# First attention's v and compressed rows at the right end, taken over by the first expert pair; five ring pairs in place of six

## The chip, the cores and the metric

The kernel runs on one core of a Trainium2 chip. Its engines work side by side: TensorE (PE) multiplies matrices, VectorE (DVE) and ScalarE (ACT) do elementwise work and read the matrix results out of PSUM, GpSimd (POOL) does small elementwise work, and SyncE (SP) issues nearly all transfers between HBM and the on-chip memory (SBUF), which 16 DMA engines carry out. The metric is the time of one execution in microseconds (us). Times of several runs are given as a median; a profiled execution has a time of its own.

## What is computed

One input of 256 tokens by 1024 features, float32, goes through two transformer blocks. The weights are read once from HBM. Cut to what matters here:

```python
# first block
h  = rms_norm(x);  z = h @ w_in                 # 1024 x 5664: c_q, c_kv, k_rope, dq, dk, dv, two gates
q  = rms_norm(c_q) @ w_uq;  k_nope, v = split(rms_norm(c_kv) @ w_ukv)
o_mla  = softmax(q k^T) v                        # 16 heads ("first attention")
o_diff = (softmax(q1 k1^T - bias) - lam * softmax(q2 k2^T - bias)) vd    # 8 heads ("second attention")
x  = x + (sigmoid(g_a) * o_mla + sigmoid(g_b) * o_diff) @ w_out
a  = softmax(rms_norm(x) @ router_w);  idx, gate = top_k(a^T, 32)        # 16 experts, 32 tokens each
x  = x + scatter(idx, gate * ((silu(xe @ w_gate) * (xe @ w_up)) @ w_down))   # w_*: 8.4 MB per expert each
# second block: projection, convolution, stick-breaking attention, gating unit, ffn of 4096, gated output
```

The experts' weights are 16 x 3 x 8.4 MB = 403 MB of the 490 MB that the kernel reads.

## The kernel before

The program is written with a framework that places tiles in SBUF, sets the waits and orders the instructions of each engine. In `build`, a block fixes the order on PE and POOL to the order of the text for the whole program; the others (DVE, ACT, SP) are ordered by the framework, by their place in the text and by when it expects them to be ready, except in marked blocks (`manual_schedule`). One of these covers the first projection in `mla` (DVE and ACT), one the last expert's down projection (SP too). Each engine then works through its instructions strictly in order; SP too, so an issue that waits holds up all that stand behind it.

SBUF is used from both ends: pools opened on the left stack up, pools with `side="right"` stack down from the other end, and a pool that is closed gives its place to the next one opened there; a tile placed on an old one waits until the old one's readers are done. The pools that matter, in the order in which they lie (KB per partition):

- left, for the whole program or long: `cp` (x and constants), `sm`, `fa` (32 KB: xh, xl, o_mla, o_diff), `qk` (24 KB: q and k of the first attention, then the gates `gT`, then weights);
- left, in the front only: `wsp` (three pairs of split weights of 1088 columns, 25.5 KB), `fs` (small statistics), `fd` (16 KB: d0 and d1, the second attention's q and k), `fv` (13 KB: pos_r, dist, lr, tab and the first attention's v of 8 KB), `a1` to `a3` (transposed heads, biases, logits, probabilities), `fe` (8 KB: first `ch`, the split and transposed compressed rows, later d2, the second attention's v), `a4`;
- right, in the front: `ring1`, four slots of 8 KB through which the front's weights pass;
- right, from the experts on: two slots of 16 KB where the four were, `pp` of 8 KB, and six slots `ring2` of 16 KB, which lie over the front's left pools.

The front (`front`, `mla`, `diff`) multiplies in three passes: each weight piece is split into a rounded part and the rest (`split`, `put`: one ACT cast, one DVE subtraction) and multiplied three times (`mm3`). `look` keeps `self.ahead` pieces split ahead. `tables` makes the position tables on POOL; `lam` makes the scalar lambda of the second attention from `lr`; `diff` ends with the gates, the merges, `w_out` and the router's logits; `route` picks the tokens.

In `experts` a weight pair is 2.1 MB (256 rows of w_gate or w_up, 512 rows of w_down): 12 pairs per expert, 192 in all, of which the last four are loaded as eight halves of 1.05 MB by `load`. `pload` takes the next place off the ring. If that is a pool, it goes back on the end of the ring, and the load waits for the matmuls that used the pair before; if it is a function, the place is used once, by one load of 2.1 MB or two of 1.05 MB, and does not come back:

```python
r = self.ring.pop(0)
if callable(r):
    hs = r()
else:
    self.ring.append(r)
    hs = [r.tile([128, 4096], F32, name="w", tag="w")]
```

`SLOTS` gives the first turn of the ring: a number is a slot of `ring2`, -1 one of the two wide slots, -2 the next place of `once`. The places of `once` are: xl with the upper part of `qk`; the lower 16 KB of `qk`; o_diff with o_mla. Before the change the first eleven pairs so take r2[3], once, r2[2], r2[1], once, r2[0], wide, wide, r2[4], r2[5], once, and the ring that remains has eight slots: r2[3], r2[2], r2[1], r2[0], wide, wide, r2[4], r2[5].

At the last expert (`e == 15`), after gate and up, three of the six slots are closed for the split weights of the second block; `load(0)` and `load(1)` load the two column halves of w_down, four quarters each, into the other three and into the first of them again. The two wide slots take the second block's first weights; a slot `ring3` is added after the experts and three more after the mixer.

## Time and profile before

| what | us |
|---|---|
| median of 3 runs | 1506.15 |
| lowest, highest of them | 1505.64, 1506.5 |
| the profiled execution | 1505.89 |
| its span, first to last instruction | 1504.2 |
| PE busy | 1138.1 |
| DVE busy | 475.5 |
| ACT busy | 354.8 |
| POOL busy | 133.0 |

The page cuts the span into 40 slices of 37.6 us and prints the busy share of each engine in tenths, the mean busy share of the 16 DMA engines, and the GB/s that they moved; below it follow the chain of work that ended last and the costliest groups of instructions. A row of the timeline is one instruction or a run of like ones on an engine: start, duration, engine, line of the program, what it writes and reads, how many, and in brackets how long the engine stood before and what ended that. "SPq" is SP's queue: its rows are the moments at which transfers are issued, not the transfers.

### The profile page before, as it was taken

The page shows a single profiled execution, that of the slowest core. Times are in us where ns is not written, and L with a number is a line of the kernel's source. Part 1 is how long each engine was busy: PE and PEld are TensorE (multiplying, and loading weights), DVE is VectorE, ACT ScalarE, POOL GpSimd, SP SyncE. Part 2 cuts the span into 40 slices and gives each one's busy share as a digit, 9 for nine tenths or more (in the row PEclk, how much of TensorE's full clock was granted, in tenths as well). Part 3 has the DMA queues.
Part 4 walks back from the last instruction along what each step waited for, and adds up shares of the span by engine and source line. Part 5 has one row for each costly group of instructions (what it writes and reads, how often), then busy time and mean ns, then how long its engine had stood idle before and what let it go on. Part 6 is the DMA issues. An engine that isn't in the chain of part 4 may idle for free.

```text
span 1504.2 us, 16611 instructions
## 1 busy us (share of the span) xinstructions
PE 1138.1 (76%) x6821; PEld 627.1 (42%) x6821; DVE 475.5 (32%) x969; ACT 354.8 (24%) x644; POOL 133.0 (9%) x181
## 2 busy tenths in 40 slices
PE   7999999885655566556565555656556899999998
PEld 6777897431111121111111111111111597889986
DVE  6987787410000000000000000000000477655456
ACT  5565655100000010000000000000000455554444
POOL 4613111000000000000000000000000134011010
PEclk9999999998688787887877888787877999999999
DMA  7533339999999999999999999999999972655520
GB/s 250 184 109 103 111 117 357 426 426 427 427 427 427 424 427 428 427 427 429 426 427 427 427 427 427 427 427 427 427 427 418 360 262 92 216 173 192 198 110 29
DMA packets 74842, 492.61 MB, mean 327 GB/s; under 512 B 5593, under 2 KB 10014, under 8 KB 50446
## 3 DMA queue, kind: packets, MB, share of 16 engines
q1 hardware_dynamic: 74366, 490.69, 80.7%
q8 instruction: 53, 0.87, 0.2%
q0 software_dynamic: 400, 0.86, 0.2%
q14 instruction: 23, 0.19, 0.0%
HBM read 490.48 MB, written 1.05 MB: 327 GB/s over the span
## 4 chain that ended last, share of the span: by engine, by line
DMA 50%; PE 37%; DVE 6%; issue 2%; ACT 1%; SPq 1%; POOL 1%; ACTq 0%; DVEq 0%
DMA w<-in_expert_w_down_dram 17%; DMA w<-in_expert_w_gate_dram 17%; DMA w<-in_expert_w_up_dram 15%; PE tr L1213 5%; PE mm L209 5%; PE mm L210 5%; PE mm L211 5%; PE acc L210 2%; PE acc L211 2%; PE acc L209 2%; DVE wl L121 2%; PE su L1261 2%; SPq L1280 1%; DMA w<-in_w_in_dram 1%; PE s L740 1%
## 5 line engine op out<-in xcount | busy, mean ns | idle before, releaser
L1213 PE MATMUL tr<-w,xe 128*32 128x512 f32 x2048 | 325.5, 768 | 207.3 <-DMA w<-in_expert_w_up_dram 121.6
L1213 PEld LDWEIGHTS tr<-w,xe 128*32 128x32 f32 x2048 | 64.7, 126 | 446.9 <-issue 162.6
L1261 PE MATMUL su<-w,hT 128*32 128x512 f32 x960 | 164.1, 821 | 92.3 <-DMA w<-in_expert_w_down_dram 84.4
L121 DVE TENSOR_TENSOR wl<-w,wh 128x1024 fp32r<-128x1024 f32 (+1 forms) x157 | 193.9, 1242 | 87.6 <-ACT wh L120 86.2
L120 ACT CAST wh<-w 128x1024 fp32r<-128x1024 f32 (+1 forms) x157 | 163.3, 1048 | 114.1 <-PE mm L211 44.9
L1239 DVE SCALAR_TENSOR_TENSOR hd<-tr,re,sg 128x512 f32<-128x512 f32 x16 | 12.0, 750 | 508.6 <-PE tr L1213 507.7
L1250 ACT ACTIVATE yh<-su,cols 128x512 fp32r<-128x512 f32 x17 | 11.7, 687 | 565.4 <-PE su L1261 528.8
L209 PE MATMUL mm<-xh,wh 128*128 128x256 f32 x448 | 128.7, 287 | 0.9 <-DVE x L1632 0.9
L210 PE MATMUL mm<-xh,wl 128*128 128x256 f32 x448 | 125.8, 281 | 0.0
L211 PE MATMUL mm<-xl,wh 128*128 128x256 f32 x448 | 125.8, 281 | 0.0
L1261 PEld LDWEIGHTS su<-w,hT 128*32 128x32 f32 x960 | 31.4, 132 | 209.4 <-DMA w<-in_expert_w_down_dram 134.3
L1251 DVE SCALAR_TENSOR_TENSOR yl<-su,cols,yh 128x512 fp32r<-128x512 f32 x17 | 12.8, 751 | 272.5 <-ACT yh L1250 272.5
L209 PEld LDWEIGHTS mm<-xh,wh 128*128 128x128 f32 x448 | 84.4, 188 | 4.0 <-issue 2.3
L210 PEld LDWEIGHTS mm<-xh,wl 128*128 128x128 f32 x448 | 84.5, 189 | 0.3
L211 PEld LDWEIGHTS mm<-xl,wh 128*128 128x128 f32 x448 | 84.4, 188 | 0.0
L1237 ACT ACTIVATE sg<-tr,re 128x512 f32<-128x512 f32 x16 | 11.0, 687 | 269.6 <-PE tr L1213 264.3
L209 PE MATMUL mm<-wh,xh 128*128 128x512 f32 (+1 forms) x140 | 57.7, 412 | 0.7 <-ACT wh L120 0.5
L1368 POOL TENSOR_SCALAR_AFFINE_SELECT m_gt<-ones 128x128 f32<-128x128 f32 x1 | 0.3, 287 | 647.6 <-DMA w<-in_expert_w_down_dram 647.6
L210 PE MATMUL mm<-wh,xl 128*128 128x512 f32 (+1 forms) x140 | 54.1, 386 | 0.0
L211 PE MATMUL mm<-wl,xh 128*128 128x512 f32 (+1 forms) x140 | 54.0, 385 | 0.0
L209 PE MATMUL acc<-wh,fhl 128*128 128x512 f32 x128 | 50.0, 391 | 0.0
L211 PE MATMUL acc<-wl,fhl 128*128 128x512 f32 x128 | 49.9, 390 | 0.0
(455 smaller groups left out, 1514.1 us busy)
## 6 DMA issues: line engine op xcount, KB each, us to landing
w<-in_expert_w_up_dram SPq DMA_DIRECT2D x64, 2048.0 KB
w<-in_expert_w_gate_dram SPq DMA_DIRECT2D x63, 2048.0 KB
w<-in_expert_w_down_dram SPq DMA_DIRECT2D x59, 2048.0 KB
w<-in_w_ff_dram SPq DMA_DIRECT2D x32, 1024.0 KB
w<-in_w_in_dram SPq DMA_DIRECT2D x29, 1024.0 KB
w<-in_expert_w_down_dram SPq DMA_DIRECT2D x10, 1024.0 KB
w<-in_w_out_dram SPq DMA_DIRECT2D x5, 1024.0 KB
w<-in_w_ple_gate_dram SPq DMA_DIRECT2D x4, 1024.0 KB
```

The lines of the kernel that those rows point to most:

```text
L120: self.nc.scalar.copy(h, src)
L121: (self.nc.gpsimd if pool else self.nc.vector).tensor_tensor(l, src, f(h), op=ALU.subtract)
L209: mm(out, ah, bh, start=start, stop=False, **kw)
L210: mm(out, al, bh, start=False, stop=False, **kw)
L211: mm(out, ah, bl, start=False, stop=stop, **kw)
L740: nc.tensor.matmul(S[:, t, :], qT[:, t * 128 : t * 128 + 128], kT, start=True, stop=True)
L1213: nc.tensor.matmul(ps[32 * j : 32 * j + 32, :], self.xe[k // 4][:, k % 4, 32 * e : 32 * e + 32], ws[k % 2][:, 0, 512 * j : 512 * j + 512], ...
L1239: nc.vector.scalar_tensor_tensor(hd, gu[1], re, sg, op0=ALU.mult, op1=ALU.mult)
L1250: nc.scalar.activation(yh, d, AF.Identity, scale=gate)
L1251: nc.vector.scalar_tensor_tensor(yl, d, gate, f(yh), op0=ALU.mult, op1=ALU.subtract)
L1261: nc.tensor.matmul(d[r : r + 32, :], hT[:, a, j, :], ws[a // 2][:, a % 2, 512 * b : 512 * b + 512], start=j == 0 and a < 2, stop=j == 3 an ...
L1280: nc.sync.dma_start(ws[j], A["expert_w_down"][0, 15, 512 * j : 512 * j + 512, 512 * b : 512 * b + 512].rearrange("(p a) n -> p a n", a=4))
```

## The change

Two pools `early` of 8 KB each are opened first on the right, and `pp` behind them, ahead of `ring1`. In the front, v lies in the first and `ch` in the second. When the experts' weights are loaded, the two are the first place of `once`: the first pair goes there in two halves of 1.05 MB. `ring2` has five slots; the first eleven pairs take early, once (xl with qk's part), r2[2], r2[1], once, r2[0], wide, wide, r2[3], r2[4], once, and the ring that remains has seven slots: r2[2], r2[1], r2[0], wide, wide, r2[3], r2[4]. At the last expert, r2[2] to r2[4] are closed and r2[0] and r2[1] stay. After the experts the two `early` pools join the ring of the second block in place of one `ring3`; after the mixer two `ring3` in place of three.

To make room, `lr` shares the place of pos_r, `lp` that of a transposed head, and the split buffers have 1024 columns, so that a weight tile of 544 columns is split row block by row block (eight pieces of 544 where there were four of 1088), with two pieces ahead in place of one.

```diff
--- before.py
+++ after.py
@@ -21,12 +21,12 @@
 PSUM = bass.MemoryType.PSUM
 
 
-R1, R2 = 4, 6
+R1, R2 = 4, 5
 
 LN_EXP = 6
 
-SLOTS = (3, -2, 2, 1, -2, 0, -1, -1, 4, 5, -2)
-WSPLIT = 1088
+SLOTS = (-2, -2, 2, 1, -2, 0, -1, -1, 3, 4, -2)
+WSPLIT = 1024
 AHEAD = 2
 T, D, NT = 256, 1024, 2
 EPS = 1e-6
@@ -310,6 +310,9 @@
         self.cms, self.wide = {}, set()
         self.cp = self.open("cp")
         self.sm = self.open("sm", 2)
+
+        self.early = [self.open("early", side="right") for _ in range(2)]
+        ppool = self.open("pp", side="right")
         r1 = self.ring = [self.open("ring1", side="right") for _ in range(R1)]
         r1 = list(r1)
         self.x = self.cp.tile([128, NT, D], F32, name="x")
@@ -325,7 +328,6 @@
             for r in reversed(r1):
                 self.close(r)
             r1 = [self.open("ring1", side="right") for _ in range(R1 // 2)]
-            ppool = self.open("pp", side="right")
             r2 = [self.open("ring2", side="right") for _ in range(R2)]
             self.wide = {id(r) for r in r1 + r2}
             once = self.once()
@@ -342,13 +344,13 @@
             ew = self.experts(rp, r2, ppool, late)
             if self.upto < 3:
                 return
-            self.ring.append(self.open("ring3", side="right"))
+            self.ring += self.early
             bm, self.ap = self.open("bm"), self.open("bq", 2)
             again = dict(ws="sg", wm="hd", ah="hT", u="yh", gl="yl", gv="sel")
             self.mix(Parts(bm, (ew, again)))
             self.close(self.ap)
             self.close(bm)
-            self.ring += [self.open("ring3", side="right") for _ in range(3)]
+            self.ring += [self.open("ring3", side="right") for _ in range(2)]
             self.ap = self.open("bf", 2)
             self.ps.turn("acc", "s", "s", "su", "o")
             self.ffn()
@@ -363,6 +365,7 @@
             both.append(tile(self.qp, "a", 4096))
             return [tile(self.fa, "xl"), tile(self.qp, "b")]
 
+        yield lambda: [tile(pool, "w") for pool in self.early]
         yield first
         yield lambda: both
         yield lambda: [tile(self.fa, "o_diff"), tile(self.fa, "o_mla")]
@@ -487,7 +490,7 @@
         wr = fp.tile([128, 2, 32], F32, name="wr")
         nc.sync.dma_start(wr[:, 0, :], A["mla_q_hnorm_w"][:, 64:].to_broadcast((128, 32)))
         nc.sync.dma_start(wr[:, 1, :], A["mla_k_hnorm_w"][:, 64:].to_broadcast((128, 32)))
-        self.lr = fp.tile([128, 4, 64], F32, name="lr")
+        self.lr = fp.tile([128, 4, 64], F32, name="lr", tag="pos_r")
         nc.sync.dma_start(self.lr, A["diff_lambda"].rearrange("o a b -> o (a b)").to_broadcast((128, 256)).rearrange(
             "p (a b) -> p a b", a=4))
 
@@ -518,7 +521,7 @@
                        allow_small_or_imprecise_dtypes=True)
         self.onr = cp.tile([16, 128], F32R, name="onr")
         nc.gpsimd.tensor_copy(self.onr, self.ones[:16, :])
-        lp = fp.tile([128, 2, 64], F32, name="lp")
+        lp = self.ap.tile([128, 2, 64], F32, name="lp", tag="qT", bufs=4)
         ls = fp.tile([128, 2], F32, name="ls")
         nc.vector.tensor_tensor(lp, lr[:, 0::2, :], lr[:, 1::2, :], op=ALU.mult)
         nc.vector.tensor_reduce(ls, lp, axis=AX.X, op=ALU.add)
@@ -573,8 +576,8 @@
         a1, a2, a3 = self.open("a1", 2), self.open("a2", 2), self.open("a3", 2)
         fe, a4 = self.open("fe"), self.open("a4", 2)
         same = lambda *tags: dict(zip(tags, tags))
-        self.fp = fb = Parts(fs, (fd, same("d0", "d1")), (fv, same("v", "dist", "tab", "pos_r", "lr")),
-                             (fe, same("d2")))
+        self.fp = fb = Parts(fs, (fd, same("d0", "d1")), (fv, same("dist", "tab", "pos_r")),
+                             (fe, same("d2")), (self.early[0], dict(v="w")), (self.early[1], dict(ch="w")))
         self.ap = Parts(a1, (a2, same("L")), (a3, same("P")), (a4, same("PT", "jj")))
         self.mla(fb)
         self.diff(fb)
@@ -601,7 +604,7 @@
             self.ahead = 0
             self.look()
             put(range(4, 8))
-            self.ahead = 1
+            self.ahead = 2
             ws = []
             tables = self.tables()
             for k in range(8):
@@ -621,7 +624,7 @@
                 pass
         self.ahead = AHEAD
         cn = fb.tile([128, NT, 512], F32, name="cn", tag="d1")
-        ch = fb.tile([128, 2, 4, T], F32R, name="ch", tag="d2")
+        ch = fb.tile([128, 2, 4, T], F32R, name="ch")
         h, l = ch[:, 0], ch[:, 1]
         self.transpose_split(cc, self.col["mla_q_norm_w"], h, l, range(4), ("tr", "o", "tr", "mm"))
         sc = self.sm.tile([128, 2, NT], F32, name="sc", tag="sc")
@@ -1223,7 +1226,7 @@
                 self.close(rp)
                 ew = self.open("ew")
             if e == 15:
-                for r in reversed(r2[3:]):
+                for r in reversed(r2[2:]):
                     self.close(r)
                     self.ring.remove(r)
                 self.wsp = self.open("wsp", 4)
@@ -1308,7 +1311,7 @@
             down(1, second, lambda j: self.fill(j % 2))
         self.fill(2)
         self.dump("x2", self.x)
-        for r in reversed(r2[:3]):
+        for r in reversed(r2[:2]):
             self.close(r)
         return ew
```

## Rows read from the trace of the kernel before

**Rows 1.** The page's slices: DMA engines busy in tenths, and GB/s.

```profile
DMA  7533339999999999999999999999999972655520
GB/s 250 184 109 103 111 117 357 426 426 427 427 427 427 424 427 428 427 427 429 426 427 427 427 427 427 427 427 427 427 427 418 360 262 92 216 173 192 198 110 29
```

**Rows 2.** The page's chain that ended last, shares of the span by engine.

```profile
DMA 50%; PE 37%; DVE 6%; issue 2%; ACT 1%; SPq 1%; POOL 1%; ACTq 0%; DVEq 0%
```

**Rows 3.** Windows: each engine's busy time, granted clock, DMA share, GB/s.

```profile
160.00:200.00 40.00, 38.94 (x320) 35.71 (x320) 32.70 (x94) 22.45 (x62) 5.97 (x4) 1.00 0.39 128
...
227.00:251.00 24.00, 24.00 (x115) 15.88 (x114) 19.19 (x43) 13.92 (x38) 5.96 (x8) 1.00 1.00 402
251.00:255.00 4.00, 3.95 (x15) 2.29 (x14) 2.34 (x6) 2.04 (x4) 0.00 (x0) 1.00 0.09 37
256.00:288.00 32.00, 27.83 (x162) 20.17 (x165) 16.09 (x55) 9.26 (x22) 0.00 (x0) 0.89 1.00 421
...
293.00:1163.00 870.00, 536.78 (x3182) 128.90 (x3174) 51.79 (x101) 28.01 (x41) 0.79 (x1) 0.80 1.01 427
```

**Rows 4.** SP's timeline, 0 to 300 us: start, duration, line, transfer, count.

```profile
48.30 0.50 SPq L334 DMA_DIRECT2D wpl<-in_w_ple_proj_dram  x1
54.47 133.35 SPq L104 DMA_DIRECT2D w<-in_w_in_dram  x16
227.02 0.35 SPq L294 DMA_DIRECT2D w<-in_expert_w_gate_dram  x1
...
254.38 0.33 SPq L299 DMA_DIRECT2D w<-in_expert_w_gate_dram  x1
282.62 0.33 SPq L294 DMA_DIRECT2D w<-in_expert_w_down_dram  x1
290.88 8.40 SPq L294 DMA_DIRECT2D w<-in_expert_w_gate_dram  x4
```

**Rows 5.** Waits of SP's queue, 195 to 300 us: total, times, longest.

```profile
SPq L299 <- DVE mhl L121: 17.3, 1, 17.3
```

**Rows 6.** PE's timeline at the first expert, 278 to 293 us.

```profile
279.43 1.06 PE L1213 MATMUL tr<-w,xe 128*32 128x512 f32 x8
...
289.75 1.07 PE L1213 MATMUL tr<-w,xe 128*32 128x512 f32 x8
```

**Rows 7.** Windows of 2 us after the pause, last column GB/s.

```profile
254.00:256.00 2.00, 2.00 (x8) 1.25 (x8) 1.48 (x3) 1.67 (x2) 0.00 (x0) 1.00 0.41 70
256.00:258.00 2.00, 2.00 (x9) 1.61 (x9) 2.00 (x3) 1.37 (x5) 0.00 (x0) 1.00 0.91 303
258.00:260.00 2.00, 2.00 (x14) 1.77 (x13) 0.39 (x2) 1.99 (x4) 0.00 (x0) 1.00 1.06 451
```

**Rows 8.** Chain that ended last, 505 to 560 us: start, us, what.

```profile
532.73 1.97 PE su L1261 x16
...
548.10 7.05 PE tr L1213 x64
```

**Rows 9.** Groups by line and form, 0 to 30 us: count, busy, mean ns.

```profile
L121 DVE TENSOR_TENSOR wl<-w,wh 128x1088 fp32r<-128x1088 f32 x4 | 5.1, 1290 | 3.0 <-ACT wh L120 3.0
```

**Rows 10.** POOL's timeline in the front, 22.9 to 25.5 us.

```profile
23.08 1.18 POOL L480 TENSOR_TENSOR di<-pos_r,pos_c 128x256 int32<-128x256 int32 x2
```

**Rows 11.** DVE's timeline in the front, 22.7 to 29 us.

```profile
25.04 0.16 DVE L528 SCALAR_TENSOR_TENSOR nlam<-ls 128x1 f32<-128x1 f32 x1 [2.22 <-ACT ls L525]
...
27.92 0.49 DVE L205 TENSOR_SCALAR cc<-s,rx 128x272 f32<-128x272 f32 x1
```

**Rows 12.** PE's timeline in the front.

```profile
28.46 0.33 PE L153 MATMUL tr<-ident,cc 128*128 128x128 f32 x1 [1.75 <-DVE cc L205]
```

**Rows 13.** PE's timeline at the last expert.

```profile
1163.50 1.92 PE L1213 MATMUL tr<-w,xe 128*32 128x512 f32 x16 [1.78 <-DMA w<-in_expert_w_up_dram]
```

**Rows 14.** A window of the last expert's down projection, last column GB/s.

```profile
1164.00:1180.00 16.00, 11.32 (x83) 5.07 (x75) 3.48 (x5) 0.69 (x1) 1.94 (x4) 1.00 1.04 381
```

**Rows 15.** Waits of PE in the second block, longest first.

```profile
PE mm L209 <- DVE x L1632: 0.9, 1, 0.9
```

## The prediction

> **What bounds the kernel now.** I read the slices of the page first: from about the eighth to the thirtieth of 40 the DMA engines move some 427 GB/s without a break [rows 1]. The chain that ended last says the same: half of the span is DMA [rows 2]. So I split the span into three stretches by their windows. Up to about 227 us the first block's attention runs; PE has hardly a gap, and the DMA engines are busy a third of the time [rows 3]. From 227 to about 1163 us the experts' 192 weight pairs of 2.1 MB stream in. After that the second block runs, again on PE without gaps. In such a kernel a microsecond counts where it moves the stream: the time is where the stream starts to run without a pause, plus the pairs left at that moment, 4.91 us each (2.097 MB at 427 GB/s), plus the second block.
>
> So the reader should look for pauses of the DMA engines in the second stretch. There is one: from 251 to 255 us only 37 GB/s move [rows 3]. SP issues in order, and the load at 254.38 [rows 4], whose place holds the gates until the last merge has read them, stands 17.3 us [rows 5]. After that load nothing pauses: 421 GB/s from 256 to 288, 427 from 293 to 1163 [rows 3]. What keeps it running at the seam is the load at 282.62 [rows 4]: the twelfth pair, which goes into the place of the first pair as soon as PE has used that up (the eight matmuls of 279.43 and the next eight [rows 6]). The eleven pairs before it are through at 288: at 254.38 nine halves (of 1.049 MB) of 22 had been issued and had landed, 13 were left, 13.63 MB; [rows 7] give 0.14 MB up to 256, and the rest takes 13.49 MB / 421 GB/s = 32.0 us. The twelfth was in the queue by then, so the stream ran on.
>
> **The change, part by part.** *The first pair.* It now goes into the two places of v and the compressed rows. Those are read last at the end of the first attention, some 160 us, where the DMA engines move 128 GB/s of 427 [rows 3], and the framework does pull a load ahead of its turn: w_ple_proj is issued at 48.30, before 16 loads of w_in [rows 4]. So 2.1 MB leave the stretch after 227 and cost nothing where they go. Behind these two loads on SP stand w_in loads; these come every 8.3 us (16 in 133.35 [rows 4]) into four slots, so a load that is held up some microseconds is still early.
>
> *The order of the others.* By the sizes in the code the left stack ends 11 KB lower (8 for v, 1 for lr, 0.5 for lp, 1.5 for the weight splits) and each ring slot that stays keeps its address. So slot r2[3] lies no longer over the small statistics that are used to the last, only over the second attention's q and k, and can be loaded before 254.38. The wait for the gates itself is not touched. Then 11 halves instead of 13 are left at 254.38, and the eleven pairs are through 4.9 us earlier, at 283; or at 288, if the framework leaves that load in its turn.
>
> *The ring of five.* Here lies the term that decides. The first and second pair now both lie in places that are used once: their slots are not put back on the ring. The twelfth pair takes the place of the third. PE ends the third pair at 290.82 (the sixth group of eight matmuls, 289.75 + 1.07 [rows 6]); SP issued a load on that release at 290.88 [rows 4]. Before, the twelfth was issued at 282.62; now it is issued at 290.88, and PE's pace there is its own: it gathers and multiplies without waiting for weights. The DMA engines will by then have stood still since 283 (or 288). How long a load takes from issue to full flow after a pause, the rows at 254.38 show: 1.65 MB by 260 (2 us each at 70, 303 and 451 GB/s [rows 7]), as much as 3.86 us at 427, so flow from 256.14, 1.76 us after the issue. So the twelfth pair flows from 290.88 + 1.8 = 292.7 instead of 288.0: **+4.7 us**. Bounds: 3.9 (1.5 us, and 288.5) to 5.3 (2.0 us, and 287.6). The 2.1 MB that went early bring nothing, since what is late next is not a transfer but a free slot.
>
> The Trainium skill (DMA: Bandwidth & Descriptors, section Specifications) gives about 0.6 us to the first byte of a load from SP; by that alone the loss would be 3.5 us and the time 1510.1. The rows measure issue to full flow, which is what counts here, and I keep them.
>
> *The stream after that.* Pair n+7 instead of n+8 is issued when pair n is used up. The six pairs still in the queue are 29.5 us of transfer; PE's longest break in the stream is the fifth expert's, from 534.70 to the first pair used after 548.10, some 15.4 us [rows 8]. Cost 0.
>
> *The front.* The four splits of 1088 columns become eight of 544. A subtraction of 1088 takes 1.29 us [rows 9]; at half the columns I estimate 0.7, so 0.4 us more on DVE in all, 0.3 on ACT. On DVE the order there is written out: the last piece now comes behind the eleven small steps of the row scale, and PE needs it for its last step. Against that, lr shares the place of pos_r, so it loads only when POOL has read pos_r, at 24.26 [rows 10]; lambda's small steps move back, and the 2.22 us that DVE stood for them at 25.04, just ahead of the row scale [rows 11], fall away there. PE waits for DVE at this spot (1.75 us, 28.46 [rows 12]), so the sum reaches PE, and from there the router and the third pair, one to one. The gain is at most the 2.2 us; the loss is at most some 3 (DVE meets lambda's load before the scaling at 27.92 [rows 11] and waits to about 27, or the late piece and its followers add 0.7 and twice 1.2). The nearest reading, DVE's own sum, is about even: I take **+0.5**, from -2.2 to +3.
>
> *The tail.* Of the last expert's down weights, the third and fourth quarter take a ring slot that is free only when PE has used pair 188 (1163.50 + 1.92 [rows 13]); before, they had a slot freed long ago. Behind them on SP wait two loads of w_in and the other half's four. The first two quarters, 2.1 MB, are 5.5 us of transfer at 381 GB/s [rows 14] after pair 188 has landed; 1.9 of PE plus 1.8 to flow is 3.7. So the queue does not run dry: 0; were one of the two quarters through before, +1, were both, +3.7.
>
> *The second block.* One slot more at its start. PE waits there three times, 0.9 us at the longest [rows 15], none of them on a weight load: 0, at most -2.7.
>
> Sum: 1505.89 (the profiled execution) + 4.7 + 0.5 = 1511.1; the median of the runs is 0.26 above that execution: **1511.3**.
>
> **The rivals.** *The pair that went early is a net gain.* The stream has one pair less from 227 on, and runs on as before: 1506.15 - 4.9 + 0.5 = 1501.7, faster. That needs the twelfth pair in the queue before the eleventh is through, so a third pair used up some 8 us sooner (or a slot that I take for used up being given back). For it: the pause before 254.38 would be filled. Against: the times of PE in [rows 6]. Chance 0.10. *The front is shorter.* The wait of 2.22 us falls away in full: 1506.15 + 4.7 - 2.2 = 1508.6, no difference to be measured. For it: PE does wait there. Against: the late piece. 0.20. *The front is longer*, by 3: 1513.9. For it: DVE is the tight engine there; against: the load may be put far behind. 0.13. *The tail runs dry*, by 2 between these two: 1513.3; 0.07. *A ring of seven starves again and again*: if each of 15 breaks between experts cost 1 us, 1526; it would need breaks over 29.5 us where 15.4 is the longest. 0.03.
>
> The Trainium skill (Perfetto Trace Analysis, section Optimization Strategy) says that the same gap again and again on the engine that should be full can mean too few buffers. That rule speaks against this change in the form of the last rival; no such gap stands in the stream's rows now.
>
> *The change doesn't do what it says*: the early pair is issued in its turn, after w_out. Then the pairs are through at 288 instead of 283, still before 292.7, and the time is the same 1511.3; it is part of the forecast's case.
>
> **How the numbers follow.** Forecast's case 0.47, from 1509.5 to 1513. The rivals as above. A measurement of this kernel tells 0.2%, 3.0 us, from no change: faster is below 1503.1 (0.10), slower above 1509.2 (0.47 + 0.13 + 0.07 + 0.03, less 0.03 for the low edge: 0.67), the rest 0.23. The range leaves out the first rival and the last: 1506.5 to 1515.
>
> **What would show it.** In the trace after: two loads of gate halves among the w_in loads before 227; the load behind the eleventh pair not at 282 but near 291 plus the front's shift, and DMA engines idle before it for 5 to 10 us; from there 427 GB/s again to the end, shifted by about 5; the row scale without the wait of 2.2. I am wrong if the DMA engines don't pause around 285, if PE reaches the third pair earlier, or if a pause stands later in the stream.

## The result, and where the 15 us came from

| | before | after |
|---|---|---|
| median of the runs, us | 1506.33 (4 runs, 1505.64 to 1508.79) | 1521.26 (4 runs, 1520.24 to 1521.52) |
| ratio, 95% interval | | 1.0094 [1.0079, 1.0109] |
| profiled execution, us (span) | 1505.89 (1504.2) | 1521.09 (1519.4) |

The change is slower, as forecast, but by some 15 us and not by 5, and outside the range. The span grew by 15.2 us, and three places in the trace divide it: 9.3 us are lost before the first expert, 4.5 us where the stream of weights restarts, and 1.3 us behind the last pair.

The first expert's first group of eight matmuls, its sixth group (which ends the third pair), and the last pair in TensorE's timeline of the kernel after (start, duration; these answer [rows 6] and [rows 13]):

```profile
288.76 1.06 PE L1216 MATMUL tr<-w,xe 128*32 128x512 f32 x8
...
299.09 1.06 PE L1216 MATMUL tr<-w,xe 128*32 128x512 f32 x8
...
1177.38 1.92 PE L1216 MATMUL tr<-w,xe 128*32 128x512 f32 x16 [1.63 <-DMA w<-in_expert_w_up_dram]
```

The first group is 288.76 - 279.43 = 9.33 us late, the last pair 1177.38 - 1163.50 = 13.88 us. So 4.55 us were lost between them, all of it at one place. SyncE's timeline of the kernel after (start, duration, line, transfer, count; answers [rows 4]):

```profile
24.42 0.33 SPq L494 DMA_DIRECT2D lr<-in_diff_lambda_dram  x1
24.84 0.39 SPq L104 DMA_DIRECT2D w<-in_mla_w_uq_dram  x1
...
62.14 0.35 SPq L299 DMA_DIRECT2D w<-in_expert_w_gate_dram  x1
...
170.16 0.35 SPq L299 DMA_DIRECT2D w<-in_expert_w_gate_dram  x1
...
263.47 0.33 SPq L299 DMA_DIRECT2D w<-in_expert_w_gate_dram  x1
...
300.21 0.33 SPq L294 DMA_DIRECT2D w<-in_expert_w_down_dram  x1
```

The early pair is loaded early, at 62.14 and 170.16. The twelfth pair is issued at 300.21, right behind the third pair's matmuls, and that is 290.88 + 9.33: where the forecast put it, plus the front's delay. The windows show the pause in front of it (last columns: granted clock, DMA share, GB/s; answers [rows 3]):

```profile
288.00:293.00 5.00, 5.00 (x32) 2.23 (x35) 1.22 (x4) 0.47 (x1) 0.00 (x0) 1.00 0.06 25
293.00:300.00 7.00, 7.00 (x44) 2.63 (x43) 0.97 (x2) 0.95 (x2) 0.00 (x0) 1.00 0.00 0
300.00:302.00 2.00, 2.00 (x16) 0.99 (x16) 0.00 (x0) 0.47 (x1) 0.00 (x0) 1.00 0.54 106
302.00:304.00 2.00, 2.00 (x24) 0.65 (x20) 0.00 (x0) 0.00 (x0) 0.00 (x0) 1.00 0.89 352
304.00:1163.00 859.00, 525.22 (x3122) 127.04 (x3118) 51.81 (x101) 28.04 (x41) 0.80 (x1) 0.80 1.01 427
```

From 300 to 304 us 0.916 MB move, as much as 2.15 us at 427 GB/s: full flow from 301.85 on, 1.64 us after the issue. After that the stream runs at 427 GB/s to the end, as before.

The front is the surprise. VectorE's timeline there (in brackets: idle time before, and what ended it; answers [rows 11]):

```profile
22.29 0.07 DVE L540 DVE_READ_ACCUMULATOR od<-x 128x1 f32 x1
28.62 0.29 DVE L526 TENSOR_TENSOR lp<-lr 128x128 f32<-128x128 f32 x1 [6.26 <-DMA lr<-in_diff_lambda_dram]
28.83 0.16 DVE L90 TENSOR_SCALAR rs_a<-ss 128x2 f32<-128x2 f32 x1
...
31.11 0.16 DVE L98 SCALAR_TENSOR_TENSOR rx<-rs_u,rs_y 128x2 f32<-128x2 f32 x1
31.19 0.72 DVE L121 TENSOR_TENSOR wl<-w,wh 128x544 fp32r<-128x544 f32 x1
...
35.70 0.49 DVE L205 TENSOR_SCALAR cc<-s,rx 128x272 f32<-128x272 f32 x1
```

Lambda's first product stands *ahead* of the whole row scale and of the last split piece. It waits 6.26 us for rows that SyncE issued only at 24.42, after 9.9 us of waiting for GpSimd; the row scale, the piece that TensorE's last step needs, and two more pieces come behind it. The scaled rows come at 35.70 and not at 27.92 [rows 11]: 7.8 us later. ScalarE is held up too (timeline, same stretch):

```profile
22.03 1.28 ACT L528 ACT_TABLE_LOAD   x1
29.27 0.20 ACT L528 ACTIVATE ls<-ls 128x2 f32<-128x2 f32 x1 [5.96 <-DVE ls L527]
29.38 1.03 ACT L120 CAST wh<-w 128x1024 fp32r<-128x1024 f32 x1
30.42 1.28 ACT L486 ACT_TABLE_LOAD   x1
31.72 0.26 ACT L486 ACTIVATE rope<-ang 128x64 f32<-128x64 f32 x1
31.99 1.28 ACT L487 ACT_TABLE_LOAD   x1
```

TensorE's waits, 10 to 80 us (total, times, longest):

```profile
PE s L211 <- DVE wl L121: 7.3, 1, 7.3
...
PE mm L209 <- DVE v L205: 2.4, 1, 2.4
```

The first has no like in the kernel before; the second was 0.4 us there:

```profile
PE mm L209 <- DVE v L205: 0.4, 1, 0.4
```

So the questions for the chip were which edit of the front makes it late, through which engine, and what the early pair and the ring are worth without it.

### The profile page after: what moved, and what is told of

It is laid out like the page before. It is cut to its first block, busy times and chain, and to the rows that moved or that the text cites. A ratio compares the mean times of both kernels' runs of the same rounds, so it can differ in the third digit from the quotient of the medians.

```text
span 1519.4 us, 16634 instructions
## 1 busy us (share of the span) xinstructions
PE 1139.2 (75%) x6821; PEld 629.4 (41%) x6821; DVE 476.9 (31%) x973; ACT 358.4 (24%) x650; POOL 129.0 (8%) x181
## 3 DMA queue, kind: packets, MB, share of 16 engines
HBM read 490.48 MB, written 1.05 MB: 324 GB/s over the span
## 4 chain that ended last, share of the span: by engine, by line
DMA 49%; PE 41%; DVE 6%; ACT 2%; issue 1%; POOL 1%; ACTq 0%; SPq 0%; DVEq 0%
DMA w<-in_expert_w_up_dram 20%; DMA w<-in_expert_w_down_dram 19%; DMA w<-in_expert_w_gate_dram 8%; PE tr L1216 5%; PE mm L209 5%; PE mm L210 5%; PE mm L211 5%; PE su L1264 3%; PE acc L210 2%; PE acc L211 2%; PE acc L209 2%; DVE wl L121 2%; PE s L743 1%; DMA pos_c<-in_positions_dram 1%; PE tr L209 1%
## 5 line engine op out<-in xcount | busy, mean ns | idle before, releaser
L1216 PE MATMUL tr<-w,xe 128*32 128x512 f32 x2048 | 321.8, 761 | 211.7 <-DMA w<-in_expert_w_up_dram 123.6
```

The lines of the kernel that those rows point to most:

```text
L1216: nc.tensor.matmul(ps[32 * j : 32 * j + 32, :], self.xe[k // 4][:, k % 4, 32 * e : 32 * e + 32], ws[k % 2][:, 0, 512 * j : 512 * j + 512], ...
```

## The experiments

Each ratio is to executions of the kernel before that were made beside that run; their medians lie between 1506.33 and 1507.86 us, so a median of the table less 1506.33 is not the loss. The column "us" is (ratio - 1) x 1506.3, with the interval's ends behind. The last column and all rows come from the one profiled execution, which can lie off the median: 2.2 us under it in after_lr_own, 1.4 over it in before_front.

| kernel | median, us | ratio, 95% interval | us | first expert group at |
|---|---|---|---|---|
| after | 1521.26 | 1.0094 [1.0079, 1.0109] | 14.2 (11.9 to 16.4) | 288.8 |
| after_lr_own | 1516.08 | 1.0058 [1.0041, 1.0074] | 8.7 (6.2 to 11.1) | 282.9 |
| after_sp_waits | 1514.04 | 1.0042 [1.0026, 1.0059] | 6.3 (3.9 to 8.9) | 282.5 |
| after_lr_late | 1518.86 | 1.0072 [1.0056, 1.0089] | 10.8 (8.4 to 13.4) | 287.4 |
| after_lp_pool | 1519.91 | 1.0084 [1.0071, 1.0098] | 12.7 (10.7 to 14.8) | 287.9 |
| before_lr_shared | 1513.28 | 1.0037 [1.0024, 1.0049] | 5.6 (3.6 to 7.4) | 285.6 |
| before_1024 | 1509.19 | 1.0016 [1.0006, 1.0025] | 2.4 (0.9 to 3.8) | 282.1 |
| before_front | 1515.19 | 1.0051 [1.0037, 1.0065] | 7.7 (5.6 to 9.8) | 290.7 |
| before_nlam_pool | 1507.07 | 1.0003 [0.9994, 1.0012] | 0.5 (-0.9 to 1.8) | 279.7 |
| after_1088 | 1513.28 | 1.0039 [1.0025, 1.0053] | 5.9 (3.8 to 8.0) | 280.4 |
| early_again | 1510.32 | 1.0023 [1.0013, 1.0033] | 3.5 (2.0 to 5.0) | 283.6 |
| early_again_tail | 1510.40 | 1.0020 [1.0010, 1.0029] | 3.0 (1.5 to 4.4) | 282.3 |
| early_1088 | 1508.05 | 1.0003 [0.9994, 1.0012] | 0.5 (-0.9 to 1.8) | 280.2 |

### Which edit makes the front late

**after_lr_own**: lambda's rows in a place of their own.

```diff
-        self.lr = fp.tile([128, 4, 64], F32, name="lr", tag="pos_r")
+        self.lr = fp.tile([128, 4, 64], F32, name="lr")
```

> The changed kernel, with lambda's rows lr in 1 KB of their own instead of in the place of the position row. Theory (the shared place): lr's load no longer waits for GpSimd's reading of the position row, so it is issued near 12 us, the scaled rows cc are written near 28 us and not 36 us, and the whole 9.3 us by which the first expert group came later (288.76 against 279.43) goes back: 1521.3 - 9.3 = 1512 us, range 1511 to 1513.5; the third pair is then used near 290 us, and the twelfth pair issued near 291 us. Rival (the pieces of 544 columns and the two pieces taken ahead make the front late): the front stays late, 1521 us. A cause of half and half would read 1516 us.

1516.08, what a cause of half and half would read; the theory's 1512 is missed. The shared place costs about 5.5 us (14.2 - 8.7), not all 9.3. The first group comes at 282.9, still 3.4 us late, and these waits of TensorE stay:

```profile
PE s L211 <- DVE wl L121: 2.6, 1, 2.6
PE mm L209 <- DVE v L205: 2.4, 1, 2.4
```

**before_1024**: the finer pieces alone, on the kernel before.

```diff
-WSPLIT = 1088
+WSPLIT = 1024
...
-            self.ahead = 1
+            self.ahead = 2
```

> The kernel before with the finer pieces alone: split pieces of at most 1024 columns (so the compressed projection goes in eight of 544, not four of 1088) and two pieces taken ahead there. With lr in its own place the changed kernel's first expert group still came 3.5 us late (282.9 against 279.4), with a wait of 2.4 us of TensorE for VectorE's v rows near 54 us, because VectorE's order has a reduction ahead of the scaling of v. Theory (this order comes from the finer pieces): 1507 + 3.5 = 1510.5 us, with that wait of 2.4 us in the trace. Rival (it comes from the early pair's loads or from v's new place): 1507 us, the wait 0.4 us as in the kernel before.

1509.19: slower by 2.4 us (3.5 was expected), with the first group 2.6 us late and the same two waits (2.5 and 2.4 us) in its trace. The rival is out: neither wait needs the early pair's loads or v's new place. The second wait comes from VectorE's order. In the kernel before, these rows of v are scaled ahead of a reduction (VectorE's timeline):

```profile
43.61 0.48 DVE L205 TENSOR_SCALAR v<-mm,rc 128x256 f32<-128x256 f32 x1
44.01 1.74 DVE L675 TENSOR_REDUCE ssq<-od 128x16 f32<-128x1536 f32 x1
```

and in before_1024 behind it:

```profile
44.69 1.74 DVE L675 TENSOR_REDUCE ssq<-od 128x16 f32<-128x1536 f32 x1
46.35 0.47 DVE L205 TENSOR_SCALAR v<-mm,rc 128x256 f32<-128x256 f32 x1
```

The run changes the width of the pieces and the number taken ahead together; which of the two costs what was not measured apart.

**before_lr_shared**: the shared place alone, on the kernel before.

```diff
-        self.lr = fp.tile([128, 4, 64], F32, name="lr")
+        self.lr = fp.tile([128, 4, 64], F32, name="lr", tag="pos_r")
```

> The kernel before, with one change: lr shares the position row's place. Theory: this alone makes the front late by about 9 us: 1506.3 + 9 = 1515 us (1512 to 1517), since nothing after the front has slack for it. Rival (the shared place only costs together with the finer pieces or the early pair's loads): 1506 to 1508 us.

1513.28, slower by 5.6 us: the shared place is enough by itself. 9 was too much, since the finer pieces' share was in it. VectorE's timeline shows the same picture, the product of lambda one step inside the row scale, and the scaled rows 5.5 us later than before (33.45 against 27.92):

```profile
19.99 0.17 DVE L90 TENSOR_SCALAR rs_a<-ss 128x2 f32<-128x2 f32 x1
28.38 0.29 DVE L523 TENSOR_TENSOR lp<-lr 128x128 f32<-128x128 f32 x1 [8.22 <-DMA lr<-in_diff_lambda_dram]
28.59 0.16 DVE L93 TENSOR_SCALAR rs_i<-rs_a 128x2 int32<-128x2 int32 x1
...
33.45 0.49 DVE L205 TENSOR_SCALAR cc<-s,rx 128x272 f32<-128x272 f32 x1
```

**before_front**: both, and lambda's product in a place of the q rows, as in the change.

```diff
+        lp = self.ap.tile([128, 2, 64], F32, name="lp", tag="qT", bufs=4)
```

> The kernel before with all of the change's edits of the front but none of the early pair: lr in the position row's place, lambda's products in a place of the q rows, pieces of at most 1024 and two taken ahead. Theory (the parts add): what these edits cost the changed kernel, 1521.3 - 1513.3 = 8.0 us, they cost here too: 1515 us (the two parts measured alone add up to 6.3 + 2.2 = 8.5). Rival (the early pair's loads, which stand behind lr's wait in SyncE's queue, are what makes it dear): 1510 to 1513 us.

1515.19: 7.7 us, against 5.6 + 2.4 = 8.0 for the parts and 14.2 - 5.9 = 8.3 for what undoing them gives back below. The parts add, within intervals of some 2 us either way. (In its one trace the first group is 11.3 us late, where the traces of the two parts give 6.2 + 2.6 = 8.8.)

### Through which engine

**after_sp_waits**: SyncE waits as in the change, but for a load that nobody reads.

```diff
-        self.lr = fp.tile([128, 4, 64], F32, name="lr", tag="pos_r")
+        self.lr = fp.tile([128, 4, 64], F32, name="lr")
...
+        again = fp.tile([128, T], I32, name="again", tag="pos_r")
+        nc.sync.dma_start(again, A["positions"].to_broadcast((128, T)))
```

> lr in its own 1 KB as above, but where lr's load stood a second, unread load of the position row goes into the position row's place, so that SyncE's queue is held up until GpSimd has read the row (about 24.4 us), while lambda's rows come early. It tells the two waits apart. Theory A (VectorE's and ScalarE's wait for lambda carries most): SyncE alone costs at most the 1.5 us that the later wait of TensorE near 54 us added, so 1512 to 1513.5 us. Theory B (SyncE's queue carries it: the weights behind the wait come 10 us late): about 1521 us.

SyncE does wait as long (its queue's waits, 8 to 60 us):

```profile
SPq L497 <- POOL di L483: 10.1, 1, 10.1
```

and the time is 1514.04, 0.5 us over theory A's range but no slower than with lr in its own place and no wait of SyncE's (1516.08); the first group comes at 282.5 and 282.9. The weights that come ten microseconds later are still early: in both runs TensorE's waits from 10 to 80 us are for VectorE's work and the input, none for a weight load. Theory B, 1521, is out.

**after_lr_late**: the other half; SyncE runs on, lambda's rows come late.

```diff
-        nc.sync.dma_start(self.lr, A["diff_lambda"]...
+        nc.gpsimd.dma_start(self.lr, A["diff_lambda"]...
```

> The changed kernel with lr's load issued from GpSimd's queue instead of SyncE's: lr still waits for the reading of the position row, but SyncE's queue runs on. Theory A (VectorE's wait carries most): lr lands between 26 and 29 us, VectorE stands until then ahead of the scaling, and the time stays at 1518 to 1521 us. Theory B (SyncE's queue carries it): the front comes back, 1512 us.

1518.86, as theory A has it. VectorE stands until 26.9 (waits, 10 to 40 us):

```profile
DVE lp L526 <- DMA lr<-in_diff_lambda_dram: 8.6, 1, 8.6
```

Lambda's rows were there 1.7 us sooner than in the kernel after (26.88 against 28.62), and the first group 1.4 us sooner. With after_sp_waits, it is the engines that read the late rows, VectorE and behind it ScalarE, that carry the loss, not the queue that loads them.

**after_lp_pool**: the reader moved. Lambda's product, sums and last step go to GpSimd; the late load stays.

```diff
-        nc.vector.tensor_tensor(lp, lr[:, 0::2, :], lr[:, 1::2, :], op=ALU.mult)
-        nc.vector.tensor_reduce(ls, lp, axis=AX.X, op=ALU.add)
+        nc.gpsimd.tensor_tensor(lp, lr[:, 0::2, :], lr[:, 1::2, :], op=ALU.mult)
+        for n in (32, 16, 8, 4, 2):
+            nc.gpsimd.tensor_tensor(lp[:, :, :n], lp[:, :, :n], lp[:, :, n : 2 * n], op=ALU.add)
+        nc.gpsimd.tensor_tensor(ls, lp[:, :, 0], lp[:, :, 1], op=ALU.add)
...
-        nc.vector.scalar_tensor_tensor(self.nlam, ls[:, 1:2], -0.2, ls[:, 0:1], op0=ALU.add, op1=ALU.subtract)
+        nc.gpsimd.tensor_scalar(self.nlam, ls[:, 1:2], -0.2, None, op0=ALU.add)
+        nc.gpsimd.tensor_tensor(self.nlam, self.nlam, ls[:, 0:1], op=ALU.subtract)
```

> The changed kernel, lr still in the position row's place and still loaded late, but lambda's products, sums and last step are on GpSimd, behind its other work, and its exponential on ScalarE comes behind the front's other steps. Nobody on VectorE or ScalarE ahead of the row scale reads the late rows. Theory (the place of the late data's reader in the engines' orders is what costs, not the late load): the front's loss falls to that of the finer pieces, the wait of 7.3 us goes to some 2.6 us, and the time is that of the run with SyncE's wait alone, 1514 to 1515 us. Rival (the late load costs by SyncE's queue and whoever needs what stands behind it): 1519 to 1521 us.

1519.91: the expected time was missed by 5 us, and the time is the one that the rival named, though the first projection did as the theory says. VectorE's and GpSimd's timelines:

```profile
28.78 0.49 DVE L205 TENSOR_SCALAR cc<-s,rx 128x272 f32<-128x272 f32 x1
```

```profile
60.58 0.46 POOL L526 TENSOR_TENSOR lp<-lr 128x128 f32<-128x128 f32 x1
```

The scaled rows come at 28.78 instead of 35.70, and the wait of 7.3 us is 2.0. But now ScalarE's exponential stands ahead of a split piece near 58 us, and GpSimd reaches lambda only at 60.58. ScalarE's and TensorE's waits, 60 to 290 and 55 to 290 us:

```profile
ACT ls L530 <- POOL ls L529: 4.9, 1, 4.9
```

```profile
PE mm L209 <- ACT wh L120: 2.9, 1, 2.9
```

The first group comes 5.0 us later than in after_lr_own. Of these, 2.9 are the wait behind ScalarE's exponential; the rest is in two waits of TensorE for VectorE, one for a split piece (0.9 us, which the kernel before and the kernel after have too) and one in the choice of the experts' tokens (1.2 us), and was not followed up. The run doesn't decide as it was meant to: it shows that the delay of the scaled rows goes when the reader goes, and that part of the loss comes back because the next reader again stands ahead of work that TensorE needs. The rival's reason, SyncE's queue, has only after_sp_waits against it. How much of the change's loss is VectorE's wait and how much ScalarE's stays open.

**before_nlam_pool**: only lambda's last step, on the kernel before, goes to GpSimd, by the last three lines of the diff above.

> The kernel before, with lambda's last step on GpSimd instead of VectorE, where it stood 2.22 us one step ahead of the row scale's last. It measures by itself what the prediction took as the largest possible gain. Theory: VectorE's second split piece then waits for ScalarE's piece at about 25.9 us all the same, so the scaled rows come only about 0.5 us earlier: 0 to 1 us faster, no difference to be measured. Rival (the wait reaches TensorE one to one): 2.2 us faster, ratio 0.9985.

The same time as before, 0.5 us slower (interval -0.9 to 1.8). VectorE's timeline:

```profile
23.05 0.16 DVE L98 SCALAR_TENSOR_TENSOR rx<-rs_u,rs_y 128x2 f32<-128x2 f32 x1
...
25.99 1.23 DVE L121 TENSOR_TENSOR wl<-w,wh 128x1024 fp32r<-128x1024 f32 x1 [0.65 <-ACT wh L120]
...
27.33 0.49 DVE L205 TENSOR_SCALAR cc<-s,rx 128x272 f32<-128x272 f32 x1
```

The row scale's last step starts 2.07 us earlier (25.12 before) and the scaled rows come 0.59 us earlier (1.0 if one counts from lambda's product, which stands 0.41 us later in this trace); the rest is taken back by ScalarE's piece. The 2.22 us of [rows 11] were not to be had: the interval leaves room for 0.9 at most.

### What the early pair and the ring are worth

**after_1088**: the three edits of the front undone; left are the early pair and the ring of five.

```diff
-WSPLIT = 1024
+WSPLIT = 1088
...
-        self.lr = fp.tile([128, 4, 64], F32, name="lr", tag="pos_r")
+        self.lr = self.ap.tile([128, 4, 64], F32, name="lr", tag="qT", bufs=4)
...
-            self.ahead = 2
+            self.ahead = 1
```

> The changed kernel with the three edits of the front that the early pair doesn't need undone: lr loads into a place of the q rows that is empty then, the pieces are 1088 wide again and one is taken ahead. Left of the change: the early pair and the ring of five. Theory: the front is that of the kernel before (first expert group near 279.5 us), the twelfth pair goes into the third pair's place and is issued near 291 us, and the time is 1507 + 4.7 (restart of the stream) + 1 (tail) = 1512 to 1513 us. Rival (the places or loads of the early pair make the front late): 1515 us or more, first expert group near 283 us.

1513.28, 0.3 us over the expected range: 5.9 us over the kernel before. The first group comes at 280.4, the twelfth pair is issued at 291.89, and the stream stands (windows):

```profile
282.00:284.00 2.00, 2.00 (x13) 0.82 (x12) 0.48 (x1) 0.00 (x0) 0.00 (x0) 1.00 1.04 434
284.00:293.00 9.00, 9.00 (x55) 3.82 (x58) 0.97 (x2) 1.01 (x3) 0.00 (x0) 1.00 0.10 24
296.00:1160.00 864.00, 538.35 (x3146) 128.82 (x3138) 51.80 (x101) 28.02 (x41) 0.79 (x1) 0.79 1.01 427
```

**early_again**: lr in its own place, and the early pair's slots go back into the ring.

```diff
             hs = r()
+            if r is self.twice:
+                self.ring.append(r)
...
-        yield lambda: [tile(pool, "w") for pool in self.early]
+        self.twice = lambda: [tile(pool, "w") for pool in self.early]
+        yield self.twice
...
-        self.lr = fp.tile([128, 4, 64], F32, name="lr", tag="pos_r")
+        self.lr = fp.tile([128, 4, 64], F32, name="lr")
...
-        ring, self.ring = [r for r in self.ring if r in r2], [r for r in self.ring if r not in r2]
+        ring, self.ring = [r for r in self.ring if r in r2], [r for r in self.ring if r not in r2 and r is not self.twice]
```

> As the run with lr in 1 KB of its own, but the early pair's two slots go back into the ring after their first use, so the ring has eight pairs again and the twelfth pair goes into the first pair's place. Theory (the place of the twelfth pair sets the restart of the stream): it is issued near 286 us instead of 294.3 us, and the time falls by about 8 us, from 1515 to 1507 us. Rival (a ring of seven starves again and again, or the stream is bound elsewhere): the time follows the first issue by less than 3 us, 1512 us or more.

1510.32: 5.2 us less than with the slots used once (8.7 - 3.5), not 8; the time lies between the theory's and the rival's. The missing part shows in the windows: with the twelfth pair through, the next place comes free only at the third pair (issue at 295.09), because the second pair's place is still used once:

```profile
292.00:294.00 2.00, 2.00 (x16) 0.80 (x18) 0.00 (x0) 0.47 (x1) 0.00 (x0) 1.00 0.33 135
294.00:296.00 2.00, 2.00 (x13) 0.82 (x12) 0.48 (x1) 0.00 (x0) 0.00 (x0) 1.00 0.00 0
```

**early_again_tail**: at the last expert the early slots take quarters as well.

```diff
+        ring += self.early
+
         def load(b):
```

> The same, and at the last expert the early pair's two slots also take quarters of its down projection, so that six and not four quarters lie ready, as in the kernel before. Theory (the second half of the last down projection waits for a quarter's slot): 1.3 us less than the run before it, 1505.7 us; the 2.1 us wait of TensorE for a quarter's load at the end of the last expert falls away. Rival (nothing waits there that the second block doesn't hide): the same time as the run before it.

The same as the run before it, 1510.40 against 1510.32, and TensorE's waits for quarters add up to 2.7 us in both. The theory of the tail is out; the rival holds.

**early_1088**: the edits of after_1088, early_again (but for lr's place) and early_again_tail together. Of what the change does to the stream, the early load alone is left; v, the compressed rows, lr and lp keep places other than before.

> The changed kernel with lr in a place of the q rows, pieces of 1088 and one taken ahead, and the early pair's slots going back into the ring and taking quarters at the last expert: everything undone but the early loads. The stream is then one pair (4.9 us) ahead of the kernel before. Theory (places, not the start, limit the stream: all eleven are full near 284 us, the twelfth pair is issued near 283.5 us and through near 290 us, and the thirteenth must wait until the third pair has been used, near 292 us, and flows near 293.7 us, against 292.9 us in the kernel before): the head start is given back, 1507 to 1508.5 us. Rival (a pair loaded earlier is a pair gained at the end): 1507 + 1 - 4.9 = 1503 us.

1508.05, ratio 1.0003 [0.9994, 1.0012]: the kernel before, to the measurement. A pair loaded 4.9 us ahead gains nothing that shows (0.5 us slower, interval -0.9 to 1.8); the rival, 1503, is out. The windows:

```profile
288.00:290.00 2.00, 2.00 (x14) 0.80 (x13) 0.00 (x0) 0.47 (x1) 0.00 (x0) 1.00 0.26 107
290.00:292.00 2.00, 2.00 (x13) 0.82 (x12) 0.48 (x1) 0.00 (x0) 0.00 (x0) 1.00 0.00 0
292.00:294.00 2.00, 2.00 (x19) 0.74 (x22) 0.00 (x0) 0.47 (x1) 0.00 (x0) 1.00 0.85 180
```

The stream waits from 288.5 to 293 for the thirteenth pair's place (issue at 291.61) and gives the head start back. Against after_1088 it is 5.4 us faster (5.9 - 0.5, each with its interval): that is the price of using the first place once. The quarters in the early slots, which early_1088 has besides, made no difference in the run before.

## Why the forecast was wrong, step by step

- **What bounds the kernel, and the seam: right.** Of 15.2 us in the trace all but 1.3 are what moved the stream: 9.33 us before its first expert, 4.55 us at its restart.
- **The ring of five: right, mechanism and size.** +4.7 was forecast; the twelfth pair, which flowed from 288.0 before, flows from 301.85, and less the front's 9.33 that is 4.5 us. Measured by itself (after_1088 against early_1088) it is 5.4 us, with some 2.5 us of doubt either way. Flow came 1.64 us after the issue, where 1.76 had been read and 1.8 used.
- **The early pair brings nothing, since what is late next is a free slot: right,** and early_1088 shows it by itself. The rival that counted a pair gained falls. The pause is even longer than forecast, some 13.5 us (288.3 to 301.85) where 5 to 10 had been named: the first eleven pairs were through no later than before, though the front was 9.3 us late, and that gained nothing either.
- **The front, +0.5 with at most +3: this step failed.** It measured +9.3 in the trace; its edits alone cost 7.7 us (before_front), 5.6 of them by the shared place (before_lr_shared) and 2.4 by the finer pieces (before_1024). Three parts of it failed:
  - *"lambda's small steps move back".* They did not move back. The product stands at the head of the row scale after as before; the planner that orders VectorE did not put it behind the load that had become late. Its place could have been read in VectorE's timeline of the kernel before, just behind the scale's first step; the forecast looked only at lambda's last step, next to the wait of 2.22 us:

```profile
20.22 0.28 DVE L523 TENSOR_TENSOR lp<-lr 128x128 f32<-128x128 f32 x1
```

  - *The bound of 3.* It named the right danger, VectorE meeting the late load, but put the meeting at the scaling, behind the row scale. It is met ahead of it, so what counts is when the rows come less when the product ran before. With the shared place alone (before_lr_shared) the product comes 28.38 - 20.22 = 8.2 us later, of which 5.5 arrive at the scaled rows: most of the rest is the stand of 2.22 us for lambda's last step, which came behind the product and which the delay fills. In the kernel after it is 28.62 - 20.22 = 8.4 us at the product and 7.8 at the scaled rows, because the finer pieces add their part there. The landing, too, was put at about 27; the load took 28.62 - 24.42 = 4.2 us from issue to its reader.
  - *The finer pieces, "about even".* The pieces were sized rightly (0.72 us for 544 columns, 0.7 estimated), and the late piece behind the row scale (twelve small steps in the trace, not eleven) does hold up TensorE, by 2.5 us in before_1024; the scaled rows come 1.2 us later there (29.11 against 27.92). But VectorE's order behind them changed as well: a reduction now comes ahead of v's rows, and TensorE waits 2.4 us for them, where it waited 0.4. The forecast had no term for that. Alone the finer pieces cost 2.4 us.
- **The gain of up to 2.2 us: not there.** The wait does fall away (lambda's last step at 31.83 waits for nothing), but with the shared place alone (before_lr_shared) it is the late rows that have taken its time, and before_nlam_pool shows that without it nothing is gained even when the rows are early.
- **SyncE's queue.** The forecast didn't price lr's 9.9 us at the head of SyncE's queue. By after_sp_waits that omission cost nothing that shows.
- **The tail, 0: open.** The profiled run lost 1.3 us between the last pair and the end (15.2 - 13.9). Two more slots there changed nothing, so the slots are not shown to be its cause. Nor is 1.3 us clear of the scatter: from the last pair's start to the end it is 340.5 to 341.8 us in the five traces with the old tail (before, before_1024, before_lr_shared, before_front, before_nlam_pool) and 340.7 to 342.8 us in the six with the new one (after, after_lr_own, after_sp_waits, after_lr_late, after_lp_pool, after_1088).

With lambda's product waiting 6.26 us, the row scale behind it, whose data had lain ready since 22.4, did not start. The Trainium skill (PSUM — Partial Sum Buffer, section Engine vs sequencer instructions) says that the queues of ScalarE, VectorE and GpSimd are strictly first in, first out; the trace agrees.

No version beat the kernel before. early_1088 and before_nlam_pool, both at 1.0003, are level with it.

## What to carry to other kernels

When data come later, look up in the trace where their first reader stands in its engine's order and what stands behind it there: the new landing less the reader's old time is how late the reader gets (8.2 us here), less the stands behind it that this fills (5.5 us were left at the scaled rows, 5.6 in the time), and a planner need not move the reader. Before loading ahead, look whether the stream waits next for transfers or for free places: here it was places, and a pair loaded ahead gained nothing. And before counting a wait as a gain, look for the next wait behind it: a stop of 2.22 us was worth 0.6 to 1.0 us at the scaled rows and nothing at the end.

## What the runs showed of the hardware

- A load of lambda's rows, 1 KB to each of 128 partitions, took 4.2 us from its issue by SyncE to its reader (24.42 to 28.62); it took 4.3 us in before_lr_shared, 4.9 in before_front, and 3.8 in after_lr_late, where GpSimd issued it.
- The mean granted clock of TensorE, of stretches at 2.4 and at 1.2 GHz, is 0.79 from 20 to 36 us in the kernel after, where TensorE stood 7.3 us, and 0.89 in the kernel before. But it is 0.79 in after_1088 as well, which has no such stop, so the difference is not shown to come from the stop, and what it costs was not measured apart. The windows of after, before and after_1088:

```profile
20.00:36.00 16.00, 7.74 (x48) 6.90 (x47) 8.02 (x24) 9.97 (x17) 8.53 (x21) 0.79 0.33 110
20.00:36.00 16.00, 13.38 (x75) 11.29 (x74) 11.97 (x46) 9.16 (x23) 10.77 (x33) 0.89 0.60 197
20.00:36.00 16.00, 12.51 (x64) 10.87 (x63) 10.84 (x38) 8.34 (x20) 10.87 (x33) 0.79 0.58 195
```

- ScalarE's order of functions has a price of its own: three ACT_TABLE_LOAD of 1.28 us stand between 20 and 34 us in the kernel after, where the kernel before has one, because lambda's exponential comes ahead of the sine. before_1024 has three there too (from 18 us on), before_lr_shared one: the new order comes with the finer pieces, not with the shared place. In the kernel after, VectorE's last split piece ahead of the scaled rows waits 0.92 us for ScalarE behind two of these loads; in before_1024 it does not wait. The Trainium skill (ScalarE activation tables: per-element evaluation and per-set limits, section What a function is on this engine) gives 1283 ns for one such switch, and the rows agree.
